# First layer: one latent tile's first products by gathered rows, ahead of the context's; second layer: splits two ahead, gathered sums added at another place

## The chip, the cores and the metric

The kernel runs on one core of one Trainium2 chip. The metric is the device time of one execution in microseconds (us). Engines: TensorE multiplies matrices, VectorE and ScalarE work on tiles, GpSimd does part of the splits and issues the gathers, SyncE issues the other DMAs.

## The reference

Two layers of a diffusion backbone work on 512 latent tokens and 256 context tokens of 1,024 numbers each. Every layer is a norm, a token mixer (attention and recurrences; latents read the context), a residual, a second norm, an expert FFN and a residual. The second layer doesn't need the context's FFN any more, but its mixer needs the context that the first layer's FFN leaves:

```
h = modulate(x, norm_w[layer, 1], sh2, sc2)
s = einsum('nhpd,hpkd->nhpk', (h @ w_q), keys)       # 8 heads, 2 halves, 128 keys each
s_top, i_top = top_k(s, 16)                          # 16 best of each half
best, pos = top_k(s_top[0] + s_top[1], 16)           # 16 of the 256 pairs
idx  = i_top[0] * 128 + i_top[1]  at pos             # one of 16,384 experts
gate = softmax(best)
act  = gelu(einsum('nd,nhkd->nhk', h, u_tab[idx]))
x = x + g2 * einsum('nhk,nhkd->nd', gate * act, v_tab[idx])
```

Each token thus uses 8 x 16 = 128 of 16,384 experts, each with a row of 1,024 in `u_tab` and one in `v_tab`, all in 32-bit floats.

## The kernel before, in words

The FFN is done in two ways beside each other. **Dense**: for a set of latent tokens, all 16,384 experts are computed in 128 steps of 128 experts ("expert j"). A first product (u, lines 1846 to 1856) is 24 matmuls, three for each of eight blocks of 128 numbers, since both operands are split into a high and a low part (`split`: the high part is a rounding copy on ScalarE, L226; the rest is a subtraction on GpSimd or VectorE, L229; lines 246, 247 and 249 are the three matmuls). GELU follows on ScalarE (L1855). Its result is multiplied by the gates that `spread` has placed: one-hot matrices ohA and ohB of the two halves of an expert's number, multiplied on TensorE (L1692) into a staging tile that goes to DRAM (G); ohB is built by VectorE and ScalarE in turn (`OH = "va"`). Most first products are done while the top-k and the spreading run and wait in DRAM (AD): 96 of 128 in the first layer, 80 in the second; the generator `u_step` does one whenever enough "price" has gathered (`UP`). The second products are in `peer_out`: for each expert the activation is weighed by its gates (`weigh`, L1896), split (wh, wl), the row block of values is split (vh, vl), and matmuls add into PSUM (lines 1960 to 1962 in the first layer, whose six accumulators are rolled over every few experts into the latents at L1886; lines 1976 to 1979 in the second). One expert is split ahead of the one that is multiplied.

**By gathers** (`sparse`, lines 1697 to 1739): a tile of 128 tokens has, for each of its 128 chosen experts, one indirect DMA issued by GpSimd that fetches one row for every token (`ga`, 128 x 1024, 0.5 MB), one dot product with the token rows on VectorE (L1727) into a column of `sact`, then GELU, a product with the gate, and again 128 gathers and 128 scaled sums on VectorE (L1737) into `sacc`. `add_tok` transposes sacc on TensorE (L235) and adds it to the stream (L1749); the context's sums pass through DRAM first. The gathers go through a ring of buffers (`NS`: four in the first layer, six in the second, and one more, `NX`, while peer_out runs).

Which tokens go which way: in the first layer (`GT[0] = 0`) all 512 latent tokens are dense and the context's two tiles (256 tokens) are gathered; in the second (`GT[1] = 2`) latents 256 to 511 are gathered and 0 to 255 dense. In the first layer the context's rows are so spread over the latents' dense FFN, and in the second the two gathered tiles over the dense ones.

The order: the program is written as generators. `s.gens` is the list of gathering generators, and `s.pull(n)` takes n steps of the first one in the list; it is called beside the top-k and u_step (`R0`) and after each expert in peer_out (`s.rate`, what is left divided by the experts left). At the end of peer_out `s.pull(1 << 20)` takes all that remains. This program order, with a scheduler that runs the program in a model and arranges each engine's instructions, sets what stands in each engine's queue; an engine takes its queue in order. The gathers carry an anchor (`issue_after`), an instruction behind which they must stand. The stretches of the span are: 950 to 1885 us first products of the first layer, 1885 to 2880 its second products, then the second layer's norm, mixer and retrieval, 3770 to 4330 its first products, 4330 to 5238 its second, and the end.

Names in the rows: `u`, `acc`, `o`, `hs`, `g` are tiles in PSUM (in the rows of L1692 the placed gates); `xl` latents, `xc` context; `htok` token rows; `c_all` constants; `hh`, `hl` the split stream and `whi`, `wlo` the split u-weights; `vraw`, `vh`, `vl` values and their split; `rh`, `rl` the values' last 256 columns, split apart in the first layer.

## Time and profile before

| | |
|---|---|
| median of 3 runs | 5307.02 us (5298.75 to 5309.9) |
| profiled execution | 5302.26 us |
| its span | 5300.4 us |
| mean granted TensorE clock | 0.899 |
| busy: TensorE, VectorE, GpSimd, ScalarE | 4334.2, 4082.6, 2884.6, 1986.3 us |
| first products (lines 246, 247, 249), both layers | 3 x 2048 matmuls, 761.8 + 748.6 + 758.1 us |
| gathers of u-rows, of v-rows | 512, 512 |
| dot products, sums on VectorE | 765.6, 748.6 us |

TensorE has 82% of the span and VectorE 77%, but not in the same places: each stretch has its own bound, so the shares say little, and a table of busy times by stretch says more. The durations of VectorE's and GpSimd's instructions vary with what runs beside them. In rows of groups the second number behind the bar is the mean of one in ns, the idle time is that of the engine just before these instructions, and what ended it stands behind the arrow.

### The profile page before, as it was taken

The numbers are of one execution on the slowest core, as the hardware profiler recorded it, in microseconds if no ns is written. First come the engines' busy times: TensorE is split into PE (matmuls) and PEld (weight loads), VectorE is DVE, ScalarE is ACT, GpSimd is POOL, SyncE is SP. The second block draws the span as 40 slices with busy tenths as digits, with TensorE's granted clock in tenths as the row PEclk, the third lists the DMA queues.
The fourth block names the chain that finished last, engine by engine and source line by source line (L and its number), as shares of the span: only waits on it lengthen the run. The fifth ranks groups of instructions, "written<-read, shape, count | busy, mean of one in ns | idle before, by whom it ended". The sixth has DMA issues, their size and how long they took to land. (4 is left out here: it accounts for less than half of the span.)

```text
span 5300.4 us, 71968 instructions
## 1 busy us (share of the span) xinstructions
PE 4334.2 (82%) x25323; PEld 3508.9 (66%) x25323; DVE 4082.6 (77%) x7744; ACT 1986.3 (37%) x3944; POOL 2884.6 (54%) x1967
## 2 busy tenths in 40 slices
PE   7899988788889978998999998978867765377775
PEld 5777766576668867776777766866756664265563
DVE  4665668899998868777787764644899869977788
ACT  3544442235555632222223463433325542122222
POOL 2232223775567756565654212424566677878775
PEclk8899988899999989999999996989978888688887
DMA  5431124777778888777886110022477789999887
GB/s 201 153 102 62 52 75 154 237 265 248 246 263 306 301 298 292 287 276 274 302 292 230 48 46 9 2 108 97 145 246 248 273 313 358 353 321 331 313 315 277
DMA packets 450409, 1155.52 MB, mean 218 GB/s; under 512 B 42112, under 2 KB 185856, under 8 KB 446464
## 3 DMA queue, kind: packets, MB, share of 16 engines
q1 hardware_dynamic: 302304, 612.94, 33.6%
q0 software_dynamic: 147744, 537.99, 28.2%
q8 instruction: 200, 3.28, 0.2%
q14 instruction: 161, 1.32, 0.1%
HBM read 1052.20 MB, written 98.57 MB: 217 GB/s over the span
## 5 line engine op out<-in xcount | busy, mean ns | idle before, releaser
L229 POOL TENSOR_TENSOR wlo<-wraw,whi 128x1024 fp32r<-128x1024 f32 x405 | 1019.3, 2519 | 1034.6 <-ACT whi L226 999.7
L1715 POOL DMA_INDIRECT ga<-in_pu,idx x512 | 668.6, 1306 | 341.8 <-DVE ga L1727 126.4
L249 PE MATMUL u<-hh,wlo 128*128 128x512 f32 (+1 forms) x2048 | 758.1, 371 | 117.7 <-POOL wlo L229 117.6
L246 PE MATMUL u<-hh,whi 128*128 128x512 f32 (+1 forms) x2048 | 761.8, 372 | 111.6 <-ACT act L1855 74.5
L1737 DVE SCALAR_TENSOR_TENSOR sacc<-ga,sact,sacc 128x1024 f32<-128x1024 f32 x508 | 748.6, 1474 | 107.6 <-DMA ga<-in_pv,idx 99.7
L1727 DVE SCALAR_TENSOR_TENSOR ga<-ga,htok 128x1024 f32<-128x1024 f32 x512 | 765.6, 1511 | 64.2 <-DMA ga<-in_pu,idx 63.9
L1715 POOL DMA_INDIRECT ga<-in_pv,idx x512 | 658.7, 1287 | 264.3 <-DVE sacc L1737 95.0
L226 ACT ACTIVATE whi<-wraw 128x1024 fp32r<-128x1024 f32 x415 | 437.1, 1054 | 859.5 <-PE u L247 469.1
L247 PE MATMUL u<-hl,whi 128*128 128x512 f32 (+1 forms) x2048 | 748.6, 366 | 0.0
L246 PEld LDWEIGHTS u<-hh,whi 128*128 128x128 f32 x2048 | 442.2, 216 | 179.6 <-ACT act L1855 89.5
L249 PEld LDWEIGHTS u<-hh,wlo 128*128 128x128 f32 x2048 | 440.9, 216 | 165.3 <-POOL wlo L229 125.5
L247 PEld LDWEIGHTS u<-hl,whi 128*128 128x128 f32 x2048 | 440.5, 215 | 38.9
L229 DVE TENSOR_TENSOR vl<-vraw,vh 128x768 fp32r<-128x768 f32 (+1 forms) x256 | 349.9, 1369 | 141.3 <-ACT vh L226 141.3
L226 ACT ACTIVATE vh<-vraw 128x768 fp32r<-128x768 f32 (+1 forms) x256 | 239.7, 945 | 287.5 <-PE acc L1961 242.1
L1692 PE MATMUL g<-ohB,ohA 128*128 128x128 f32 x1536 | 253.8, 294 | 111.0 <-DVE ohB L1690 89.5
L1692 PEld LDWEIGHTS g<-ohB,ohA 128*128 128x128 f32 x1536 | 225.2, 201 | 153.4 <-DVE ohB L1690 66.1
L1962 PE MATMUL acc<-wh,vl 128*128 128x512 f32 x768 | 307.7, 401 | 22.6 <-DVE vl L229 22.4
L1960 PE MATMUL acc<-wh,vh 128*128 128x512 f32 x768 | 292.9, 396 | 29.7 <-ACT wh L226 29.7
L1961 PE MATMUL acc<-wl,vh 128*128 128x512 f32 x768 | 305.3, 398 | 8.5 <-POOL wl L229 8.5
L1690 DVE TENSOR_SCALAR ohB<-c_all,pt 128x128 f32<-128x128 f32 x384 | 246.0, 655 | 46.5 <-PE g L1692 46.1
L229 POOL TENSOR_TENSOR wl<-ad,wh 128x512 fp32r<-128x512 f32 (+1 forms) x176 | 214.6, 1219 | 64.4 <-ACT wh L226 30.6
L1855 ACT ACTIVATE act<-u 128x512 f32<-128x512 f32 (+1 forms) x256 | 122.7, 479 | 329.9 <-PE u L249 125.7
(507 smaller groups left out, 9822.6 us busy)
## 6 DMA issues: line engine op xcount, KB each, us to landing
wraw<-in_uT SPq DMA_DIRECT2D x256, 512.0 KB, 4.5
vraw<-in_pv SPq DMA_DIRECT2D x256, 512.0 KB, 6.8
wraw<-in_ada_w SPq DMA_DIRECT2D x96, 512.0 KB, 4.8
G<-stg SPq DMA_DIRECT2D x24, 2048.0 KB, 8.6
wraw<-in_ew SPq DMA_DIRECT2D x64, 512.0 KB, 3.9
G<-G SPq DMA_DIRECT2D x32, 1024.0 KB, 6.7
wraw<-in_pwq SPq DMA_DIRECT2D x48, 512.0 KB, 3.9
AD<-act SPq DMA_DIRECT2D x96, 256.0 KB, 4.6
```

The costliest lines, as they stand in the source:

```text
L226: nc.scalar.activation(hi, x, AF.Copy)
L229: i = (lo_eng or nc.vector).tensor_tensor(lo, x, hi.bitcast(F32), OP.subtract)
L246: nc.tensor.matmul(o, a, hh[:, k], start=(k == 0), stop=False)
L247: nc.tensor.matmul(o, a, hl[:, k], start=False, stop=False)
L249: nc.tensor.matmul(o, b, hh[:, k], start=False, stop=(k == nk - 1))
L1692: nc.tensor.matmul(ps[:, n], A[:, n], B, start=True, stop=True)
L1715: nc.gpsimd.indirect_dma_start(out=ga, out_offset=None, in_=tab, in_offset=bass.IndirectOffsetOnAxis(ap=idx[:, k:k + 1], axis=0))
L1727: nc.vector.scalar_tensor_tensor(ga, ga, 1.0, htok, op0=OP.mult, op1=OP.mult, accum_out=act[:, k:k + 1])
L1737: nc.vector.scalar_tensor_tensor(acc, ga, act[:, k:k + 1], acc, op0=OP.mult, op1=OP.add)
L1960: nc.tensor.matmul(acc[d], a, wh, start=st, stop=False)
L1961: nc.tensor.matmul(acc[d], a, wl, start=False, stop=False)
L1962: nc.tensor.matmul(acc[d], b, wh, start=False, stop=sp)
```

## The change

In the first layer one latent tile, tokens 384 to 511, gets its first products by gathers: 128 gathers of u-rows and 128 dot products (a `sparse` with `half=True`, which ends after GELU and gate). Its own ring has three buffers (`NH`), and its generator is put at the head of `s.gens`, ahead of the context's. The result, gate times activation, goes to `spread` in place of the gate (`halves`, whose ohB all come from VectorE). The dense first products of this layer then cover 384 tokens (`ND`) instead of 512, the second products still 512 (`NW`); `weigh` multiplies 384 columns and uses the other 128 as they were placed. In both layers two tiles have their top-k beside the queries (`NF`; before: one in the first layer). The rings shrink from four and six buffers to three and five (`NS`), the one-hot tiles from six to four (`NE`), and `UP[0]` and `R0[0]` change. In the second layer's second products two experts are split ahead instead of one (`PD`). The sum of its gathered tile that is ready first is transposed and added after expert 101 (`LT = 100`), the other after the last expert; each has a buffer of its own.

```diff
-UP = (5.5, 4.0)
+UP = (4.0, 4.0)
 GT = (0, 2)
-R0 = (2.0, 2.5)
+HT = (1, 0)
+PD = (1, 2)
+R0 = (1.8, 2.5)
 RG = (2, 1)
...
+LT = 100
 RX = 2.0
-NE = 6
+NE = 4
...
-NS = (4, 6)
+NS = (3, 5)
+NF = (2, 2)
+NH = (3, 0)
+TB = 32
...
-    def spread(s, p, p2, p3, sp, psp, gps, pick, tb0, G):
+    def spread(s, p, p2, p3, sp, psp, gps, pick, tb0, G, oh=OH):
...
-                    if OH[c % len(OH)] == 'a':
+                    if oh[c % len(oh)] == 'a':
...
-    def sparse(s, l, p2, pick, src, done):
+    def sparse(s, l, p2, pick, src, done, half=False, pools=None):
...
-        s.nsp += 1
-        q = s.nsp % 2
+        s.nsp += not pools
+        q = 'h' if pools else s.nsp % 2
...
-            s.turn = (s.turn + 1) % len(s.gpools)
-            ga = s.t(s.gpools[s.turn], [128, D], tag='ga')
+            if pools:
+                ga = s.t(s.next_pool(pools), [128, D], tag='ga')
+            else:
+                s.turn = (s.turn + 1) % len(s.gpools)
+                ga = s.t(s.gpools[s.turn], [128, D], tag='ga')
...
-            while len(ahead) < len(s.gpools) and k + len(ahead) < 128:
+            while len(ahead) < len(pools or s.gpools) and k + len(ahead) < 128:
...
-        acc = s.t(p2, [128, D], tag='sacc')
+        if half:
+            done(act)
+            return
+        acc = s.t(p2, [128, D], tag='sacc' if l == 0 else f'sacc{q}')
...
-        ng = GT[l]
-        ND = T - 128 * ng
+        ng, nh = GT[l], HT[l]
+        NW = T - 128 * ng
+        ND = NW - 128 * nh
...
-        tiles = list(range(0, T, 128)) if ctx else list(range(ND, T, 128)) + list(range(0, ND, 128))
+        tiles = list(range(ND, T, 128)) + list(range(0, ND, 128))
...
+            late = []
...
-                    for i in range(ng):
+                    for i in range(ng + nh):
...
+                eg, gated = [], {}
+                if nh and NH[l]:
+                    hs = ee(tc.tile_pool(name=s.name("hs"), bufs=1))
+                    hr = ee(tc.tile_pool(name=s.name("hr"), bufs=NH[l]))
+                def halves():
+                    for i in range(nh):
+                        while i not in gated:
+                            s.pull(1)
+                        pk3 = s.pick[i][0:2] + (gated[i],)
+                        yield from s.spread(*eg, psm, gps, pk3, tiles[i] // TB, G, 'v')
                 def done():
                 def after(i):
                     t0 = tiles[i]
                     if t0 >= ND:
-                        s.todo += 256
-                        s.gens.append(s.sparse(l, s.sp2, s.pick[i], HT[(t0 - ND) // 128],
-                                               lambda acc: s.add_tok(psu, 'u', acc, s.xl, t0, gl)))
-                        next(s.gens[-1])
+                        half = t0 < NW
+                        def end(x):
+                            if half:
+                                gated[i] = x.rearrange("p (a b) -> p a b", a=8)
+                            else:
+                                late.append((x, t0))
+                        s.todo += 128 if half else 256
+                        own = half and NH[l]
+                        g = s.sparse(l, hs if own else s.sp2, s.pick[i], HTok[(t0 - ND) // 128], end, half,
+                                     [hr] * NH[l] if own else None)
+                        s.gens.insert(0 if own else len(s.gens), g)
+                        next(g)
                         return
                     yield from s.spread(*eg, psm, gps, s.pick[i], t0 // TB, G)
                 price, n = 0.0, 0
-                for p in s.retrieve(l, ep, tp_, pk, (psq, 'q'), (psm, 'hs'), (hh, hl), tiles, 1 if ctx else ng, done, after):
+                for p in s.chain([s.retrieve(l, ep, tp_, pk, (psq, 'q'), (psm, 'hs'), (hh, hl), tiles, NF[l],
+                                             done, after), halves()]):
                     price += p
                     if p == 0 and s.gens:
-            s.peer_out(l, ND, old, ap, psu, hd, G, AD, gl)
+            s.peer_out(l, ND, NW, old, ap, psu, hd, G, AD, gl, late)
...
         groups = [list(range(j, j + JG)) for j in range(0, 128, JG)]
...
+        with tc.tile_pool(name=s.name("po"), bufs=2) as p2, tc.tile_pool(name=s.name("pv"), bufs=1 + PD[l]) as pvp, \
+                tc.tile_pool(name=s.name("pw"), bufs=RG[l] + PW + PD[l] - 1) as pw, tc.tile_pool(name=s.name("sp3"), bufs=NX) as sp3, \
...
-                nc.vector.tensor_tensor(a3, a3, G_[:, :, j - g[0], :], OP.mult)
-                return a
+                gj = G_[:, :, j - g[0], :]
+                if ND == NW:
+                    nc.vector.tensor_tensor(a3, a3, gj, OP.mult)
+                    return a3
+                nc.vector.tensor_tensor(gj[:, 0:ND // TB], a3, gj[:, 0:ND // TB], OP.mult)
+                return gj
             def prep(j, a):
-                wh = s.t(pw, [128, ND], F32R, tag='wh')
-                wl = s.t(pw, [128, ND], F32R, tag='wl')
-                s.split(a, wh, wl, lo_eng=nc.gpsimd)
+                wh = s.t(pw, [128, NW], F32R, tag='wh')
+                wl = s.t(pw, [128, NW], F32R, tag='wl')
+                s.split(a, *[x.rearrange("p (b n) -> p b n", n=TB) for x in (wh, wl)], lo_eng=nc.gpsimd)
...
-            a0, a1 = ready(0), ready(1)
-            nxt = prep(todo[0][1], a0)
+            gated = [ready(n) for n in range(PD[l] + 1)]
+            split = [prep(todo[n][1], gated.pop(0)) for n in range(PD[l])]
             pend, cur = [], []
             for n in range(128):
-                (vh, vl), w = nxt
+                (vh, vl), w = split.pop(0)
                 load(n + LA)
                 vload(n + NV)
-                a2 = ready(n + 2)
-                if n + 1 < 128:
-                    nxt = prep(todo[n + 1][1], a1)
-                a1 = a2
+                gated.append(ready(n + PD[l] + 1))
+                if n + PD[l] < 128:
+                    split.append(prep(todo[n + PD[l]][1], gated.pop(0)))
...
-                            nc.tensor.matmul(acc[2 * t + e], b, vh[:, e * 512:e * 512 + 512], start=False, stop=sp)
+                            i = nc.tensor.matmul(acc[2 * t + e], b, vh[:, e * 512:e * 512 + 512], start=False, stop=sp)
+                    if n == LT and late:
+                        a, t0 = late.pop(0)
+                        with tc.issue_after(i.ins):
+                            s.add_tok(psu, 'u', a, s.xl, t0, gl)
                 s.pull(s.rate)
             s.pull(1 << 20)
+            for a, t0 in late:
+                s.add_tok(psu, 'u', a, s.xl, t0, gl)
```

The order of VectorE's instructions at the end of the first layer, before: the last splits of values (L229) and sums of the context (L1737), the last additions to the latents, and the additions of the two context tiles' sums to xc.

```order
L229 TENSOR_TENSOR rl_24331<-vraw_24239,rh_24330 128x256
L1737 SCALAR_TENSOR_TENSOR sacc_20943<-ga_24234,sact_1736_8267,sacc_20943 128x1024
L229 TENSOR_TENSOR vl_24327<-vraw_24239,vh_24326 128x768
...
L1886 SCALAR_TENSOR_TENSOR xl_8281<-u_24380,g_1859_8933,xl_8281 128x512
L1886 SCALAR_TENSOR_TENSOR xl_8281<-u_24388,g_1859_8933,xl_8281 128x512
L1749 SCALAR_TENSOR_TENSOR xc_24419<-o_24432,g_5380_24421,xc_24419 128x128 x4
L1749 SCALAR_TENSOR_TENSOR xc_24419<-o_24441,g_5380_24421,xc_24419 128x128 x4
L1749 SCALAR_TENSOR_TENSOR xc_24419<-o_24452,g_5380_24421,xc_24419 128x128 x4
L1749 SCALAR_TENSOR_TENSOR xc_24419<-o_24461,g_5380_24421,xc_24419 128x128 x4
```

And after: the latents' last additions are at L1923, the context's sums at L1751, the additions to xc at L1763; the second "..." leaves out 89 more sums.

```order
L1923 SCALAR_TENSOR_TENSOR xl_8281<-u_24755,g_1874_8971,xl_8281 128x512
L1751 SCALAR_TENSOR_TENSOR sacc_22181<-ga_22778,sact_1736_8267,sacc_22181 128x1024
L1923 SCALAR_TENSOR_TENSOR xl_8281<-u_24763,g_1874_8971,xl_8281 128x512
L1751 SCALAR_TENSOR_TENSOR sacc_22181<-ga_22814,sact_1736_8267,sacc_22181 128x1024
...
L1751 SCALAR_TENSOR_TENSOR sacc_22181<-ga_22817,sact_1736_8267,sacc_22181 128x1024
L1763 SCALAR_TENSOR_TENSOR xc_24794<-o_24816,g_5529_24796,xc_24794 128x128 x2
L1751 SCALAR_TENSOR_TENSOR sacc_22181<-ga_22859,sact_1736_8267,sacc_22181 128x1024
L1751 SCALAR_TENSOR_TENSOR sacc_22181<-ga_22862,sact_1736_8267,sacc_22181 128x1024
L1751 SCALAR_TENSOR_TENSOR sacc_22181<-ga_22908,sact_1736_8267,sacc_22181 128x1024
...
L1751 SCALAR_TENSOR_TENSOR sacc_22181<-ga_24692,sact_1736_8267,sacc_22181 128x1024
L1763 SCALAR_TENSOR_TENSOR xc_24794<-o_24827,g_5529_24796,xc_24794 128x128 x4
L1763 SCALAR_TENSOR_TENSOR xc_24794<-o_24836,g_5529_24796,xc_24794 128x128 x4
```

Before, the last sums stood among the splits of the last experts and only a few additions followed; after the change 92 sums of one context tile stand in a row behind the last latent addition, and the second context tile's additions (o_24827, o_24836) stand behind them.

TensorE's queue at the same place, before: the last matmul of the last expert (L1884), four times four transposes (L235) of the context's two sums, loaded again as a_5381 and a_5384, and the first matmul of the second layer's norm (L289).

```order
L1884 MATMUL u_24388<-wh_24322,rl_24331 128x512
L235 MATMUL o_24432<-c_all_63,a_5381_24430 128x128 x4
L235 MATMUL o_24441<-c_all_63,a_5381_24430 128x128 x4
L235 MATMUL o_24452<-c_all_63,a_5384_24450 128x128 x4
L235 MATMUL o_24461<-c_all_63,a_5384_24450 128x128 x4
L289 MATMUL hs_24529<-sq_24530,c_all_63 128x256
```

After (L1921, L241 and L295 are these lines' new numbers):

```order
L1921 MATMUL u_24763<-wh_24696,rl_24705 128x512
L241 MATMUL o_24807<-c_all_63,a_5530_24805 128x128 x4
L241 MATMUL o_24816<-c_all_63,a_5530_24805 128x128 x4
L241 MATMUL o_24827<-c_all_63,a_5533_24825 128x128 x4
L241 MATMUL o_24836<-c_all_63,a_5533_24825 128x128 x4
L295 MATMUL hs_24904<-sq_24905,c_all_63 128x256
```

TensorE's order is the same at this place; the transposes still stand ahead of the norm, and the last eight read what the last of the context's sums on VectorE leave.

TensorE's queue in the second layer's second products, where the first gathered tile's sum (`sacc`) is transposed, before: behind the matmuls of an expert (L1979), and ahead of the first product of a later one (L246, L247).

```order
L1979 MATMUL acc_8026_38107<-vh_39307,wl_39304 128x512
L1979 MATMUL acc_8027_38108<-vh_39307,wl_39304 128x512
L235 MATMUL u_39232<-c_all_63,sacc_36984 128x128 x4
L235 MATMUL u_39241<-c_all_63,sacc_36984 128x128 x4
L246 MATMUL u_39269<-hh_31545,whi_39204 128x256
L247 MATMUL u_39269<-hl_31546,whi_39204 128x256
```

After: the transposes (L241) stand behind the matmuls of expert 101 (L2020), and more second products follow (L2017).

```order
L2020 MATMUL acc_8174_38480<-vh_42988,wl_42985 128x512
L2020 MATMUL acc_8175_38481<-vh_42988,wl_42985 128x512
L241 MATMUL u_43063<-c_all_63,sacc_7966_37359 128x128 x4
L241 MATMUL u_43072<-c_all_63,sacc_7966_37359 128x128 x4
L2017 MATMUL acc_8172_38478<-vh_43016,wh_43012 128x512
L2017 MATMUL acc_8173_38479<-vh_43016,wh_43012 128x512
```

The transposes have moved from about a third of the way to a place where the first sum has been complete for long.

VectorE at the end of the second layer, before: sums (L1737) between the last splits of values, and then the last ones of the second tile ahead of its additions to the latents (L1749).

```order
L1737 SCALAR_TENSOR_TENSOR sacc_41526<-ga_43324,sact_6931_33297,sacc_41526 128x1024
L229 TENSOR_TENSOR vl_43775<-vraw_43686,vh_43774 128x1024
L1737 SCALAR_TENSOR_TENSOR sacc_41526<-ga_43358,sact_6931_33297,sacc_41526 128x1024
L229 TENSOR_TENSOR vl_43796<-vraw_43744,vh_43795 128x1024
...
L1737 SCALAR_TENSOR_TENSOR sacc_41526<-ga_43715,sact_6931_33297,sacc_41526 128x1024
L1749 SCALAR_TENSOR_TENSOR xl_8281<-u_43811,g_6588_31818,xl_8281 128x128 x4
```

After: the last split of values, the last six dot products of the second tile (L1738), the product with the gate (L1741), and the first sum (L1749); its other 127 sums follow.

```order
L235 TENSOR_TENSOR vl_44157<-vraw_44127,vh_44156 128x1024
L1738 SCALAR_TENSOR_TENSOR ga_41730,sact_7079_33670<-ga_41730,htok_7080_33671 128x1024
L1738 SCALAR_TENSOR_TENSOR ga_41733,sact_7079_33670<-ga_41733,htok_7080_33671 128x1024
L1738 SCALAR_TENSOR_TENSOR ga_41771,sact_7079_33670<-ga_41771,htok_7080_33671 128x1024
L1738 SCALAR_TENSOR_TENSOR ga_41774,sact_7079_33670<-ga_41774,htok_7080_33671 128x1024
L1738 SCALAR_TENSOR_TENSOR ga_41798,sact_7079_33670<-ga_41798,htok_7080_33671 128x1024
L1738 SCALAR_TENSOR_TENSOR ga_41801,sact_7079_33670<-ga_41801,htok_7080_33671 128x1024
L1741 TENSOR_TENSOR sact_7079_33670<-sact_7079_33670,gate_7031_33472 128x128
L1749 TENSOR_SCALAR sacc_8965_41919<-ga_41920,sact_7079_33670 128x1024
```

Behind the last split of values stood 20 sums, and now six dot products and 128 sums do.

## Rows read from the trace of the kernel before

**Rows 1.** The table of stretches: us, busy time by engine (instructions), clock, DMA

```profile
core 0: us, PE busy (x) PEld busy (x) DVE busy (x) ACT busy (x) POOL busy (x), PEclk, DMA share, GB/s
950.00:1100.00 150.00, 125.26 (x518) 97.53 (x519) 130.30 (x284) 40.91 (x93) 124.29 (x77) 0.85 0.76 255
1100.00:1600.00 500.00, 425.51 (x2004) 348.91 (x2003) 495.45 (x1236) 243.14 (x491) 311.58 (x182) 0.93 0.75 255
1600.00:1885.00 285.00, 258.68 (x1358) 219.94 (x1356) 222.77 (x255) 169.36 (x375) 195.46 (x108) 0.97 0.83 297
1885.00:2880.00 995.00, 913.41 (x3821) 727.08 (x3822) 798.22 (x914) 266.05 (x444) 590.81 (x426) 0.97 0.80 288
4330.00:4480.00 150.00, 105.96 (x427) 82.07 (x428) 121.50 (x108) 44.23 (x65) 111.61 (x87) 0.87 0.97 347
4480.00:4580.00 100.00, 1.57 (x8) 0.98 (x7) 92.15 (x73) 1.06 (x1) 77.38 (x69) 0.53 0.99 373
4580.00:5238.00 658.00, 489.02 (x2130) 389.40 (x2131) 545.95 (x572) 187.88 (x277) 526.07 (x377) 0.86 0.91 326
```

**Rows 2.** The waits, 1885 to 2880 us: who for whom, us, times, longest

```profile
ACT vh L226 <- PE acc L1961: 242.1, 95, 6.1
```

**Rows 3.** TensorE's timeline near 1701 us: start, duration, instruction

```profile
1701.42 0.40 PE L247 MATMUL u<-hl,whi 128*128 128x512 f32 x1
1701.65 0.40 PE L249 MATMUL u<-hh,wlo 128*128 128x512 f32 x1
```

**Rows 4.** TensorE's timeline near 4100 us

```profile
4099.94 0.28 PE L246 MATMUL u<-hh,whi 128*128 128x256 f32 x1
4100.06 0.28 PE L247 MATMUL u<-hl,whi 128*128 128x256 f32 x1
```

**Rows 5.** Three lines' durations: ns, minimum/median/maximum, first and last start in us

```profile
L1727 DVE SCALAR_TENSOR_TENSOR ga<-ga,htok x512: 1195/1214/8399, 959.3 to 4952.0; 128x1024 f32<-128x1024 f32 x171
L1737 DVE SCALAR_TENSOR_TENSOR sacc<-ga,sact,sacc x508: 1257/1285/4046, 1426.9 to 5263.1; 128x1024 f32<-128x1024 f32 x170
L1690 DVE TENSOR_SCALAR ohB<-c_all,pt x384: 286/336/3207, 1205.1 to 4303.5; 128x128 f32<-128x128 f32 x192
```

**Rows 6.** Groups on VectorE, 1100 to 1885 us: busy, mean ns, idle before

```profile
L1690 DVE TENSOR_SCALAR ohB<-c_all,pt 128x128 f32<-128x128 f32 x256 | 155.2, 621 | 15.1 <-PE g L1692 14.9
```

**Rows 7.** Groups on GpSimd, 960 to 1060 us

```profile
L1715 POOL DMA_INDIRECT ga<-in_pu,idx x38 | 55.7, 1466 | 11.6 <-issue 5.8 <-DVE tv L1552 1.4 <-DVE cd L1582 1.1
L229 POOL TENSOR_TENSOR wlo<-wraw,whi 128x1024 fp32r<-128x1024 f32 x10 | 24.3, 2433 | 0.2
```

**Rows 8.** DMA issues, 960-1060 and 4480-4580 us: count, median us to landing

```profile
ga<-in_pu,idx POOLq DMA_INDIRECT x38, 5.9
...
ga<-in_pv,idx POOLq DMA_INDIRECT x64, 6.2
```

**Rows 9.** Groups on GpSimd, 4480 to 4580 us

```profile
L1715 POOL DMA_INDIRECT ga<-in_pv,idx x64 | 72.7, 1136 | 21.3 <-issue 18.0 <-DVE sacc L1737 3.1 <-DMA ga<-in_pv,idx 0.3
```

**Rows 10.** VectorE's timeline, 5230 to 5275 us

```profile
5236.91 1.21 DVE L229 TENSOR_TENSOR vl<-vraw,vh 128x1024 fp32r<-128x1024 f32 x1
5238.05 26.37 DVE L1737 SCALAR_TENSOR_TENSOR sacc<-ga,sact,sacc 128x1024 f32<-128x1024 f32 x20
```

**Rows 11.** TensorE's timeline at two transposes, with the idle time before

```profile
4579.89 1.33 PE L235 MATMUL u<-c_all,sacc 128*128 128x128 f32 x5 [98.43 <-DVE sacc L1737]
...
5264.47 1.97 PE L235 MATMUL u<-c_all,sacc 128*128 128x128 f32 x8 [22.22 <-DVE sacc L1737]
```

**Rows 12.** The waits, 4330 to 5270 us

```profile
ACT wh L226 <- PE acc L1977: 330.1, 100, 12.1
...
DVE vl L229 <- ACT vh L226: 126.3, 51, 9.1
```

**Rows 13.** Groups on VectorE, 4330 to 5270 us

```profile
L1737 DVE SCALAR_TENSOR_TENSOR sacc<-ga,sact,sacc 128x1024 f32<-128x1024 f32 x249 | 350.7, 1408 | 11.8 <-DMA ga<-in_pv,idx 6.5
```

**Rows 14.** The page's groups over the whole span

```profile
L1690 DVE TENSOR_SCALAR ohB<-c_all,pt 128x128 f32<-128x128 f32 x384 | 246.0, 655 | 46.5 <-PE g L1692 46.1
```

25 lines of the change are left out of this document (11 added, 14 removed).

## The prediction, on record before the changed kernel ran

> **What bounds the kernel now.** I read the table of stretches first, then the waits of the two expert stretches, then single durations, and last the order of the built program. In the table [rows 1] the first layer's first products (950 to 1885 us) belong to VectorE: 495.5 of 500 us busy from 1100 to 1600, 848.6 of 935 us over the whole. Its second products (1885 to 2880 us) belong to TensorE: 913.4 of 995 us busy at a granted clock of 0.97, while VectorE works 798.2 us; ScalarE waits 242.1 us there, in 95 waits, for TensorE to give buffers back [rows 2]. In the second layer's second products (4330 to 5238 us, 908 us) VectorE has 759.6 us, GpSimd 715.1 us and the DMA engines a share of 0.91 to 0.99, while TensorE works less than two thirds. Two things stand out there. TensorE stops for 98.4 us, because the transposes of the first gathered sum stand in its queue ahead of the next experts [rows 11]; VectorE stays busy meanwhile (92.2 of 100 us), so the stop isn't lost for it. And VectorE waits 126.3 us for ScalarE's part of a split, which itself waits 330.1 us for TensorE [rows 12]: the split is only one expert ahead.
>
> **The change, part by part.** The sum is made against the profiled execution's own 5302.3 us (span 5300.4, 1.9 us around it); the median of the runs is 4.8 us above that.
>
> A. First layer, first products. A first-product matmul of 512 columns starts every 0.23 us, one of 256 every 0.12 us [rows 3, 4]; I put 384 columns midway, 0.175 us. The 96 experts of this stretch save 96 x 24 x 0.055 = 127 us of TensorE. But VectorE binds here, and it gets more: counted in the built order, 266 dot products and sums of gathered rows stand ahead of the first weighing, where 245 stood, and 64 one-hots come over from ScalarE. At the undisturbed 1.29 us and 0.34 us [rows 5] that is 27 + 22 us: 898 us. Of its 86 idle us, 37 would be left if the stretch kept its length. I take 0. Ends: -28, if VectorE gets the 99% it has from 1100 to 1600 us (898/0.99 = 907), +45 if the 82 idle us outside that stretch stay. Top-k of a second tile beside the queries moves work inside this sum. The change adds one wait: the gathered tile's placing stands behind its last dot product, a GELU and three transposes; behind it in TensorE's queue are only that tile's 128 placing matmuls, and VectorE has context rows to take meanwhile, so nothing is added for it.
>
> The one-hot shows what the undisturbed price hides: median 0.34 us, mean 0.62 us in this stretch [rows 5, 6], with a longest of 3.2 us. The Trainium skill (SBUF — State Buffer, Who interferes with whom) says that a VectorE instruction with two SBUF inputs, or in a two-port mode, and a GpSimd instruction that reads SBUF exclude each other for the whole instruction, so whoever comes second waits it out. By that rule the added work costs its mean and A would be +18 us dearer for the one-hots (64 x 0.28); I keep the median, since the added one-hots stand behind the last weight split.
>
> B. First layer, second products. The 32 remaining first products save 32 x 24 x 0.055 = 42 us on TensorE, which binds. Gathered rows hardly change (274 in the order for 267), nor does VectorE (798 + 9 - some us for narrower weighing). Value -41. Ends: -123, if TensorE never waits (872 us), and +41, if its 82 idle us double. The spilled activations and the one tile held a step longer touch DMA and buffers that aren't short there (share 0.80).
>
> C. The end of the first layer. This is the largest new cost, and only the order shows it (the first two pairs of order rows in the section on the change). 128 more gathered rows must pass through VectorE, and the scheduler hasn't fitted them in: behind the last expert stand 92 sums of the context in one row, where there was none. The transposes of that sum stand in TensorE's queue ahead of every norm of the second layer, and on VectorE the context's additions and norms stand behind the 92. So nothing of the second layer covers them. Price of one: VectorE's own pace is 26.37/20 = 1.32 us [rows 10], when the rows have been fetched already. Here they go through a ring of four buffers. A ring of four gave 38 gathers in 100 us, 2.63 us each, beside weight splits [rows 7]; a ring of seven, with GpSimd doing nothing else, 69 in 100 us, 1.45 us each [rows 1, 9]. Rows land 5.9 to 6.2 us after the issue in both [rows 8], so fewer buffers mean a slower pace. Midway is 2.04 us: 92 x 2.04 = +188 us. Ends: 92 x 1.32 = +121 and 92 x 2.63 = +242.
>
> The Trainium skill (DMA: Bandwidth & Descriptors, Anatomy of one DMA — SWDGE (gpsimd) path) gives a DMA issued by GpSimd about 2.0 us and its bytes at 436 GB/s; an estimate from that for 512 KB is 3.2 us, and four buffers would then feed VectorE at its own pace. No row here is that short: 5.9 us at the median. That result is the fourth rival.
>
> D. Second layer, first products. Four one-hot buffers for six: VectorE's waits of 46.1 us for the placing matmul [rows 14] may grow. Value +8, ends 0 and +46 (the row doubled). Five gather buffers for six cost nothing in this stretch: rows are used far behind their landing.
>
> E. Second layer, second products. The 98.4 us stop goes, since the transposes now stand behind expert 101 (third pair of order rows); 16 transposes are hidden in TensorE's idle time. Splitting two ahead takes ScalarE's wait for TensorE off VectorE. And the stretch loses work: the order has 238 gathered rows up to the last value split where 356 stood. 118 fewer, at 1.41 us on VectorE [rows 13], 1.14 us on GpSimd [rows 9] and 0.52 MB each, leave 593 us, 581 us and 304 - 62 = 242 MB, which at 373 GB/s, the most in the table [rows 1], take 649 us. That is the floor: -259. The ceiling is the old pace without the stop, 908 - 98 = 810 us, less the 49 rows that go from outside it (356 - 69 - 238, at 1.41 us): 741 us, -167. I take 700: -208.
>
> F. The end of the second layer. What left E stands behind the last value split: 6 dot products and 128 sums, where 20 sums took 26.4 us and TensorE waited 22.2 us for them [rows 10, 11]. Its ring has six buffers, near the seven that gave 1.45 us: 134 x 1.45 - 26 = +168. Ends: at 1.32 us +151, at 2.04 us +247.
>
> Sum: 0 - 41 + 188 + 8 - 208 + 168 = +115, so 5302 + 115 = 5417 us.
>
> **Rivals.** 1, faster: gathered rows arrive as fast as VectorE takes them, and freed of 118 of them the second layer's experts run at the DMA floor: -41 + 121 + 8 - 259 + 151 = -20, 5282 us. For it: in the stop VectorE was 92% busy on gathers alone. Against: a DMA share of 1 was only reached there. It decides once E takes under 669 us (-239).
> 2, slower still: the ring sets both ends (2.63 and 2.04 us) and E keeps its old pace: -41 + 242 + 8 - 167 + 247 = +289, 5591 us. For it: rows 7 and 8. Against: the 24 us of weight splits in rows 7, which the ends don't have.
> 3, the first end is hidden behind the second layer's norms: +115 - 188 = -73, 5229 us. Against it stands TensorE's queue.
> 4, both ends at VectorE's pace, the rest as forecast: -41 + 121 + 8 - 208 + 151 = +31, 5333 us. For it: 1.32 us in rows 10; against: those 20 rows had been fetched ahead by seven buffers.
>
> **How the numbers follow.** Forecast 0.55, with a range of its own of 5320 to 5530 (the ends of A to F, added as squares, and a fifth off). Rival 1 0.12, rival 2 0.17, rival 3 0.05, rival 4 0.11. The range 5270 to 5580 leaves out rival 3, a third of rival 1 and about half of rival 2: 0.17. 0.2% of the time is 11 us, about what a measurement can tell from no change. Faster by more: rival 3 and most of rival 1, 0.15. Within: 0.04, from rivals 1 and 4. Slower: 0.81.
>
> **What would show it.** Right: on VectorE, a row of some 92 sums behind the first layer's last expert with TensorE idle beside it, for about 190 us (2 us a sum), and 128 sums at the end with a wait of TensorE near 190 us; no stop of 98 us, and VectorE's wait for ScalarE's value split far under 126 us; second products near 955 us in the first layer, near 700 us in the second. Wrong: C, if those sums go at 1.3 us or something of the second layer runs beside them; E, if the experts still take 740 us, or under 669; A, if the first products shrink by more than 28 us, for then TensorE's saving counted where I let VectorE bind.

## The result and the profile after

The changed kernel takes 5475.14 us (median of 4 runs, 5468.24 to 5491.29), the kernel before 5302.89 us in runs beside it: a ratio of 1.032, 95% interval 1.0294 to 1.0347. The profiled execution spans 5472.2 us, 171.8 more than before. The forecast was 5417 us.

For the comparison I cut both spans at the same six events, read from the timelines: the first dot product, the first and the last second product (`acc`) of the first layer, the first matmul of the second layer's norm, and in the second layer again the first dot product and the first and last second product. The table of stretches of the kernel before, cut so (us, busy time by engine with instructions, granted clock, DMA share, GB/s; the mixer between the layers is left out):

```profile
core 0: us, PE busy (x) PEld busy (x) DVE busy (x) ACT busy (x) POOL busy (x), PEclk, DMA share, GB/s
959.00:1892.00 933.00, 806.33 (x3871) 664.36 (x3869) 850.87 (x1776) 454.01 (x959) 624.90 (x359) 0.93 0.78 267
1892.00:2875.00 983.00, 909.26 (x3801) 723.89 (x3802) 789.99 (x904) 264.30 (x441) 590.81 (x426) 0.97 0.80 289
2875.00:2884.00 9.00, 6.49 (x34) 4.79 (x34) 7.03 (x20) 0.72 (x2) 0.00 (x0) 1.00 0.42 135
3834.00:4337.00 503.00, 336.32 (x2123) 314.33 (x2123) 459.60 (x911) 218.92 (x463) 345.30 (x208) 0.82 0.78 267
4337.00:5242.00 905.00, 600.48 (x2576) 475.43 (x2576) 757.77 (x748) 233.10 (x343) 712.33 (x529) 0.82 0.93 335
5242.00:5300.00 58.00, 16.18 (x42) 7.84 (x40) 37.27 (x54) 8.68 (x14) 11.95 (x12) 0.63 0.42 156
```

The same of the changed kernel:

```profile
970.00:1969.00 999.00, 749.62 (x3876) 686.41 (x3876) 882.41 (x1992) 415.52 (x839) 630.23 (x382) 0.85 0.75 256
1969.00:2861.00 892.00, 850.13 (x3805) 705.49 (x3806) 828.68 (x912) 258.30 (x440) 613.74 (x440) 0.99 0.92 316
2861.00:3057.00 196.00, 6.10 (x30) 4.68 (x29) 130.03 (x116) 0.69 (x2) 112.12 (x94) 0.52 0.81 267
3988.00:4510.00 522.00, 341.62 (x2123) 318.52 (x2124) 468.40 (x918) 227.72 (x466) 356.43 (x213) 0.78 0.79 267
4510.00:5233.00 723.00, 569.83 (x2576) 456.02 (x2575) 607.49 (x621) 230.60 (x340) 561.36 (x406) 0.89 0.93 326
5233.00:5472.00 239.00, 16.55 (x40) 8.13 (x40) 184.69 (x176) 12.53 (x17) 153.81 (x130) 0.52 0.81 296
```

Row by row, by the events' own times (the rows are cut at whole us), the differences are the terms A to F of the prediction: +66, -91, +188, +19, -182, +181 us. What is left of the 171.8, -9 us, is the start (+10) and the mixer between the layers (-19); over all the kernels below these two vary between 949 and 970 us and between 932 and 962 us.

The end of the first layer is the largest. TensorE's timeline there (the number in brackets is the idle time before; [rows 11] are its like):

```profile
3054.34 1.94 PE L241 MATMUL o<-c_all,a 128*128 128x128 f32 x8 [186.23 <-DMA a<-AC]
3056.78 1.65 PE L295 MATMUL hs<-sq,c_all 128*128 128x256 f32 x3 [0.51 <-ACT sq L294]
```

and what VectorE and GpSimd did in those 196 us (groups, answering to [rows 9, 13]):

```profile
L1751 DVE SCALAR_TENSOR_TENSOR sacc<-ga,sact,sacc 128x1024 f32<-128x1024 f32 x96 | 123.3, 1284 | 57.7 <-DMA ga<-in_pv,idx 56.3 <-DVE sacc L1751 0.3
...
L1726 POOL DMA_INDIRECT ga<-in_pv,idx x93 | 112.1, 1206 | 69.1 <-DVE sacc L1751 53.8 <-issue 10.7 <-DMA ga<-in_pv,idx 4.6
```

96 sums take 123.3 + 57.7 = 181 us, 1.89 us each. VectorE waits for the rows to land, and GpSimd waits for VectorE to give a buffer back: a ring that is too small shows itself by these two waits together. At the second layer's end, TensorE's timeline and the two groups:

```profile
5434.44 1.97 PE L241 MATMUL u<-c_all,sacc 128*128 128x128 f32 x8 [201.49 <-DVE sacc L1751]
```

```profile
L1751 DVE SCALAR_TENSOR_TENSOR sacc<-ga,sact,sacc 128x1024 f32<-128x1024 f32 x127 | 163.2, 1285 | 28.2 <-DMA ga<-in_pv,idx 25.0
...
L1726 POOL DMA_INDIRECT ga<-in_pv,idx x128 | 151.6, 1185 | 40.7 <-issue 37.8 <-DMA ga<-in_pv,idx 1.7 <-DVE sacc L1751 1.2
```

Here a sum takes (163.2 + 28.2)/127 = 1.51 us, and GpSimd waits only 2.9 us for others: 1.19 us of issuing and 0.3 us between two issues make 1.5 us. With six buffers it is GpSimd's pace, with four the ring's. The stop of 98.43 us [rows 11] is gone: the first sum's eight transposes follow the matmuls ahead of them without a wait (timeline, first line), and of the waits of [rows 12] these are left:

```profile
5091.47 1.91 PE L241 MATMUL u<-c_all,sacc 128*128 128x128 f32 x8
...
ACT wh L232 <- PE acc L2018: 269.4, 95, 8.3
DVE vl L235 <- ACT vh L232: 90.7, 47, 6.7
```

### The profile page after: what moved, and what is told of

Same layout as the page of the kernel before. It is cut to its first block, busy times and chain, and to the rows that moved or that the text cites. A ratio compares the mean times of both kernels' runs of the same rounds, so it can differ in the third digit from the quotient of the medians.

```text
span 5472.2 us, 72624 instructions
## 1 busy us (share of the span) xinstructions
PE 4190.1 (77%) x25331; PEld 3495.3 (64%) x25331; DVE 4284.9 (78%) x8066; ACT 1951.8 (36%) x3828; POOL 3024.3 (55%) x2095
## 5 line engine op out<-in xcount | busy, mean ns | idle before, releaser
L235 POOL TENSOR_TENSOR wlo<-wraw,whi 128x1024 fp32r<-128x1024 f32 x405 | 996.9, 2465 | 913.9 <-ACT whi L232 876.5
L1751 DVE SCALAR_TENSOR_TENSOR sacc<-ga,sact,sacc 128x1024 f32<-128x1024 f32 x508 | 711.6, 1401 | 112.1 <-DMA ga<-in_pv,idx 104.0
L255 PE MATMUL u<-hh,wlo 128*128 128x384 f32 (+1 forms) x2048 | 692.6, 339 | 117.1 <-POOL wlo L235 116.9
L1738 DVE SCALAR_TENSOR_TENSOR ga<-ga,htok 128x1024 f32<-128x1024 f32 x512 | 732.0, 1443 | 29.7 <-DMA ga<-in_pu,idx 29.3
L252 PE MATMUL u<-hh,whi 128*128 128x384 f32 (+1 forms) x2048 | 687.8, 336 | 71.1 <-ACT act L1892 61.4
L253 PE MATMUL u<-hl,whi 128*128 128x384 f32 (+1 forms) x2048 | 681.0, 333 | 0.0
L1699 PE MATMUL g<-ohB,ohA 128*128 128x128 f32 x1536 | 303.8, 335 | 177.6 <-DVE ohB L1697 127.4
L235 DVE TENSOR_TENSOR vl<-vraw,vh 128x768 fp32r<-128x768 f32 (+1 forms) x256 | 319.6, 1255 | 118.8 <-ACT vh L232 103.9
L1699 PEld LDWEIGHTS g<-ohB,ohA 128*128 128x128 f32 x1536 | 257.9, 232 | 219.2 <-DVE ohB L1697 111.8
L1726 POOL DMA_INDIRECT ga<-in_pu,idxh x128 | 159.5, 1246 | 151.7 <-DVE ga L1738 29.9
L1892 ACT ACTIVATE act<-u 128x384 f32<-128x384 f32 (+1 forms) x256 | 109.5, 428 | 340.7 <-PE u L255 197.0
```

The costliest lines, as they stand in the source:

```text
L235: i = (lo_eng or nc.vector).tensor_tensor(lo, x, hi.bitcast(F32), OP.subtract)
L252: nc.tensor.matmul(o, a, hh[:, k], start=(k == 0), stop=False)
L253: nc.tensor.matmul(o, a, hl[:, k], start=False, stop=False)
L255: nc.tensor.matmul(o, b, hh[:, k], start=False, stop=(k == nk - 1))
L1699: nc.tensor.matmul(ps[:, n], A[:, n], B, start=True, stop=True)
L1726: nc.gpsimd.indirect_dma_start(out=ga, out_offset=None, in_=tab, in_offset=bass.IndirectOffsetOnAxis(ap=idx[:, k:k + 1], axis=0))
```

## The experiments

Stage lengths in us from each profiled execution, cut as above: A to F are the six rows of the tables of stretches, and E+F is the sum of the last two. The ratio is to the kernel before, run beside it on the same chip (5303 to 5316 us there), with its 95% interval.

| kernel | A | B | C | D | E | F | E+F | median | ratio |
|---|---|---|---|---|---|---|---|---|---|
| before | 933 | 983 | 8 | 503 | 905 | 59 | 963 | 5303 | 1 |
| changed | 999 | 892 | 196 | 521 | 723 | 240 | 963 | 5475 | 1.032 (1.0294 to 1.0347) |
| e1 no half tile | 993 | 965 | 8 | 521 | 741 | 228 | 969 | 5379 | 1.0141 (1.0096 to 1.0186) |
| e2 no late addition | 998 | 893 | 195 | 519 | 837 | 121 | 958 | 5478 | 1.0327 (1.027 to 1.0385) |
| e3 one split ahead | 1002 | 888 | 197 | 521 | 733 | 232 | 965 | 5488 | 1.0325 (1.0274 to 1.0376) |
| e4 price of before | 1048 | 897 | 143 | 508 | 725 | 259 | 984 | 5488 | 1.0329 (1.028 to 1.0378) |
| e5 e1, price of before | 1017 | 961 | 8 | 522 | 726 | 234 | 960 | 5380 | 1.0136 (1.0104 to 1.0168) |
| e6 e1, buffers of before | 921 | 948 | 8 | 479 | 704 | 262 | 966 | 5254 | 0.9901 (0.9879 to 0.9924) |
| e7 ring of ten | 931 | 985 | 8 | 501 | 893 | 96 | 989 | 5333 | 1.0038 (1.0017 to 1.006) |
| e8 ring of nine, not late | 932 | 991 | 8 | 504 | 973 | 31 | 1004 | 5358 | 1.0082 (1.0056 to 1.0108) |
| e9 more buffers at both ends | 996 | 877 | 152 | 525 | 816 | 129 | 945 | 5412 | 1.0191 (1.0163 to 1.0218) |
| e10 values loaded twice | 1007 | 896 | 197 | 524 | 793 | 228 | 1021 | 5547 | 1.0439 (1.0413 to 1.0466) |
| e11 e6, one top-k | 917 | 951 | 8 | 498 | 708 | 266 | 974 | 5262 | 0.9909 (0.9883 to 0.9936) |
| e12 e6, one gathered tile | 919 | 954 | 8 | 625 | 721 | 36 | 757 | 5174 | 0.9743 (0.9717 to 0.977) |

The profiled execution of e6 (5218 us) is the fastest of its five; its stages are some 36 us short of its median.

**The half-gathered tile alone (e1).**

```diff
-HT = (1, 0)
+HT = (0, 0)
```

> The changed kernel with HT = (0, 0): all four latent tiles of the first layer dense again, everything else as changed (rings, one-hot tiles, constants, second layer). Theory: in the changed trace the first layer up to the second's first norm costs 173 us more than before (first products +77 with their start, second products -92, the end +188), and all of it comes from the half-gathered tile; the second layer's FFN costs +18 us. So about 5300 us, 5285 to 5330, a span from the first layer's last second product to the next norm under 15 us instead of 196, and a second layer as in the changed kernel (second products near 723 us, the end near 239 us). Rival: the smaller rings and the second layer's new order are what costs; then 5350 us or more.

5379 us: the rival's number. Without the half tile the end C is 8 us again, as the theory had it, but A is still 60 us longer than before, and D 18 us. So the tile itself costs +6 - 73 + 188 = 121 us over A to C (96 us between the medians), and something else in the change costs the rest.

**Price or buffers (e4, e5, e6).** e4 puts the price back in the changed kernel; e5 and e6 start from e1.

```diff
 # e4
-UP = (4.0, 4.0)
+UP = (5.5, 4.0)
 # e5, on e1
-UP = (4.0, 4.0)
+UP = (5.5, 4.0)
-R0 = (1.8, 2.5)
+R0 = (2.0, 2.5)
 # e6, on e1
-NE = 4
+NE = 6
-NS = (3, 5)
+NS = (4, 5)
```

> The changed kernel with the price of a first product in the first layer put back from 4.0 to 5.5, so that the first products are spread over the whole placing instead of ending some 240 us before the second products. The built order has 295 dot products and sums ahead of the first weighing (changed: 266) and 71 behind the last expert (100). Theory: in the changed kernel TensorE has nothing beside the half tile's last dot products and its placing (a wait of 38.5 us and 87 us of placing), and with first products left beside it that time is covered: the first products' stretch falls from 1025 us to some 960 to 1000 us though it holds 29 rows more, the end from 196 to 196 - 29 x 1.92 = 140 us, and the total to 5370 to 5410 us. Rival: VectorE binds there throughout; the stretch grows by 29 x 1.29 = 37 us and only the end gets shorter: 5455 us.

> The first experiment's kernel (HT = (0, 0)) with the first layer's constants UP and R0 of before as well (5.5 and 2.0), rings and one-hot tiles still as changed. In the first experiment the first layer's first products took 993 us with no gathered tile (before: 933, changed: 999), so something else in the change costs 60 us there. Theory: the lower price ends the first products some 120 us ahead of the placing, which then runs alone; with it undone the stretch falls to 935 to 955 us, and the total from 5379 to some 5335 us. Rival: the smaller rings and the four one-hot tiles slow the placing itself (VectorE waits 60.8 us for the placing matmul there, 14.9 before); then the stretch stays at 980 us or more and the total at 5370 us or more.

> The first experiment's kernel (HT = (0, 0)) with six one-hot tiles again and four gather buffers in the first layer (NE = 6, NS = (4, 5)), price and pull as changed. Rival of the run beside it: the rings and one-hot tiles cost the 60 us; then the first products' stretch of the first layer falls to 935 to 955 us, that of the second from 521 to 505 us, and the total to some 5320 us. Theory of the price: the first layer's stretch stays at 980 us or more, and only the second layer's falls by 15 us: 5360 us.

In all three the price as a cause falls. e4 does what its rival said, in kind: 295 rows ahead in place of 266 make A 49 us longer (37 expected) and C 53 us shorter (71 sums left: 143 us, 140 expected), and nothing is won: 5488 us. First products left over didn't cover the tile's placing either; TensorE waits longer for the gathered activation than in the changed kernel (timelines of the changed kernel and of e4):

```profile
1861.22 0.47 PE L241 MATMUL hs<-c_all,sacth 128*128 128x128 f32 x1 [38.49 <-DVE sacth L1741]
...
1899.20 0.47 PE L241 MATMUL hs<-c_all,sacth 128*128 128x128 f32 x1 [81.17 <-DVE sacth L1741]
```

In e5 A grows, to 1017 us. In e6 it falls to 921 us, below before and below the 935 to 955 expected. The two waits that shrink stand on VectorE. Groups of e1, 964 to 1956 us:

```profile
L1697 DVE TENSOR_SCALAR ohB<-c_all,pt 128x128 f32<-128x128 f32 x256 | 163.9, 646 | 61.4 <-PE g L1699 60.8
L1751 DVE SCALAR_TENSOR_TENSOR sacc<-ga,sact,sacc 128x1024 f32<-128x1024 f32 x100 | 159.5, 1595 | 65.2 <-DMA ga<-in_pv,idx 64.0
```

and of e6, 959 to 1880 us:

```profile
L1751 DVE SCALAR_TENSOR_TENSOR sacc<-ga,sact,sacc 128x1024 f32<-128x1024 f32 x101 | 160.3, 1587 | 33.7 <-DMA ga<-in_pv,idx 32.7
L1697 DVE TENSOR_SCALAR ohB<-c_all,pt 128x128 f32<-128x128 f32 x256 | 148.9, 599 | 21.7 <-PE g L1699 21.4
```

39 us less waiting for the placing matmul to free a one-hot tile, and 31 us less for rows to land: 71 of the 72 us by which A differs. It isn't the fast execution of e6 that does it: e11 and e12, with the same sizes, have an A of 917 and 919 us. The two sizes weren't tried apart, nor were they put back beside the half tile.

**The second layer (e2, e3, e7, e8).**

```diff
 # e2 (and e8)
-                                late.append((x, t0))
+                                s.add_tok(psu, 'u', x, s.xl, t0, gl)
 # e3
-PD = (1, 2)
+PD = (1, 1)
 # e7 and e8: HT = (0, 0), UP = (5.5, 4.0), R0 = (2.0, 2.5), NE = 6, NF = (1, 2), and
-NX = 1
+NX = (1, 5)        # e8: (1, 4)
-NS = (3, 5)
+NS = (4, 5)
```

> The changed kernel with the first gathered sum of the second layer transposed and added as soon as it is summed (as before), so behind about the 29th expert in TensorE's queue instead of the 101st; splits stay two ahead. Its built order has 311 gathered rows up to the last value split (changed: 238) and 61 behind it (134). Theory: the stop was never lost for VectorE, the late addition only moves the rows from the stop to the end; so TensorE's stop of some 100 us is back, second products take 723 + 73 x 1.4 = 825 us, the end 239 - 73 x 1.47 = 132 us, and the total is that of the changed kernel, 5475 us, within 15. Rival: the rows fit in beside the experts without lengthening them; then the second products stay near 730 us and the total falls by about 100, to 5375 us.

> The changed kernel with PD = (1, 1): the second layer's splits one expert ahead as before, the late addition kept. Theory: the experts gain their speed from having fewer gathered rows beside them, and the second split ahead took only 36 us off VectorE's wait for ScalarE's value split (126.3 to 90.7 us); so second products of 735 to 760 us instead of 723 and 5485 to 5510 us. Rival 1: gathers and DMA set the pace whatever the split does: 5475 us, within 8. Rival 2: the split ahead is the main gain: second products over 790 us, 5545 us or more.

> First layer as before the change in all its constants; second layer as changed (splits two ahead, first sum added after expert 101) with a ring of ten gather buffers in the second products instead of six, which the scheduler uses to place 340 gathered rows up to the last value split (changed: 238) and 48 behind it (134). The end of the second layer: 239.6 - 86 x 1.47 = 113 us in every theory. Theory: in the experts' stretch VectorE is free for 116 of 723 us, and the DMA engines, at 326 GB/s there, have shown 373; 102 rows more are 53 MB, 289 MB in all: 775 to 833 us, and the total is 5303 - 963 + 888 to 946 = 5228 to 5286 us, faster than before. Rival: the DMA engines give no more than 326 GB/s beside the experts: 887 us, and 5340 us in all. Second rival: VectorE pays 1.41 us for each row: 867 us, 5320 us.

> As the run of ten buffers, but with nine and with the first sum added as soon as it is ready, so that TensorE's stop is back; the built order then has all 388 rows ahead of the last value split and none behind it. The experts' stretch moves 314 MB: 843 us at 373 GB/s, 938 us at the 335 GB/s of before; the end is some 40 us. Theory: a larger ring lets the rows catch up in the stop and the end falls away: between 5223 and 5318 us, and nearer to the run of ten buffers the less the stop costs. Rival: the stop itself is a loss of about 100 us; then it is at least 50 us slower than the run of ten buffers.

e2 is as the theory had it: the stop is back (a wait of TensorE, in e2),

```profile
PE u L241 <- DVE sacc L1751: 104.1, 1, 104.1
```

E is 837 us (825 expected), F 121 (132), and the total that of the changed kernel. In e3 E is 733 us, 10 more than in the changed kernel and just under the theory's 735 to 760, and the total of 5488 us is at the theory's lower end; by its ratio it can't be told from the changed kernel, and E+F is 965 us against 963, so that the first rival isn't excluded. e7 and e8 place 102 and 150 more rows beside the experts and lose what the end gives back. e8, at 5358 us, is above its theory's 5318 and 25 us behind e7, where its rival wanted 50: neither came out. The stretches of e7:

```profile
4345.00:5239.00 894.00, 638.91 (x2576) 491.78 (x2576) 715.80 (x737) 231.94 (x343) 700.71 (x510) 0.81 0.91 326
5239.00:5335.00 96.00, 16.06 (x42) 7.65 (x40) 73.90 (x83) 8.55 (x13) 37.72 (x38) 0.57 0.61 235
```

326 GB/s, as the first rival said, and E+F of 989 us instead of 963. Between e2, e3, e7, e8, before and changed, E+F stays within 958 to 1004 us, wherever 134 rows or none stand behind the last expert. e9 below, with a ring of eight, has 945 us; whether the larger ring gains these 18 us can't be told from one execution of each.

**What sets that sum (e10).** Of a second load of every value block nobody reads anything:

```diff
                     getattr(nc, VQ).dma_start(out=R[j], in_=pv[j])
+                    if l == 1:
+                        x = s.t(rvx, [128, D], tag='vraw2')
+                        getattr(nc, VQ).dma_start(out=x, in_=pv[j])
```

> The changed kernel with every value block of the second layer's second products loaded a second time into a tile that nobody reads (128 x 0.52 MB = 67 MB more, nothing more on the engines). Theory: second products and end together (962 us) are set by the DMA engines, whose busy time there is 866 us in the changed kernel and 866 us in the one before (share times length); 67 MB more at the 322 GB/s of both are 208 us more, so 140 to 210 us and 5615 to 5685 us in all. Rival: VectorE or the ring's round trip sets it; the DMA engines have 96 us free, and the total rises by less than 50 us.

Between the two: E+F rises by 59 us, the median by 72. The experts' stretch of e10:

```profile
4524.00:5317.00 793.00, 598.28 (x2575) 478.12 (x2575) 596.07 (x629) 233.32 (x339) 566.58 (x410) 0.84 1.01 382
```

With the extra bytes the DMA engines do bind (share 1.01, 382 GB/s), but of the 208 us that the bytes would cost at the old rate some 70% found room. So in the changed kernel they are near the limit and not at it. VectorE (792 of 963 us busy over E and F) and GpSimd (715 busy, and 71 us more between its own issues) are near it too. No one of them was shown to set the sum alone; that stays open, and e12, which takes load off all three, doesn't tell them apart.

**The ring at the first layer's end (e9).**

```diff
-NX = 1
+NX = 3
```

> The changed kernel with three more gather buffers instead of one in both layers' second products (NX = 3: six in the first layer, eight in the second). Its built order keeps 95 sums behind the first layer's last expert (changed: 100) and moves 62 rows of the second layer from the end (72 left) to the experts. Theory of the ring: the sums at the first layer's end go at 1.47 us, the pace that six buffers had at the second layer's end, instead of 1.92: 95 x 1.47 + 12 = 152 us instead of 196. Rival: the pace of 1.92 us is the DMA's or GpSimd's own there; the end stays at 185 us or more. Second layer, by the runs so far (second products and end together 958 to 1003 us wherever the rows stood): no gain, 950 to 1000 us. Total by the theory 5420 to 5450 us, by the rival 5475 us.

C is 152 us, as worked out; E+F (945 us) and the total (5412 us) lie 5 and 8 us below what was expected. The groups of e9 from 2826 to 2978 us:

```profile
L1751 DVE SCALAR_TENSOR_TENSOR sacc<-ga,sact,sacc 128x1024 f32<-128x1024 f32 x92 | 118.2, 1285 | 14.7 <-DMA ga<-in_pv,idx 12.6
...
L1726 POOL DMA_INDIRECT ga<-in_pv,idx x88 | 100.9, 1147 | 33.3 <-issue 25.6 <-DVE sacc L1751 7.7
```

(118.2 + 14.7)/92 = 1.44 us a sum, and GpSimd's wait for a buffer is 7.7 us instead of 53.8. With two buffers more the ring no longer limits.

**One top-k beside the queries (e11).**

```diff
 # on e6
-NF = (2, 2)
+NF = (1, 2)
```

> The sixth experiment's kernel (HT = (0, 0), six one-hot tiles, four gather buffers in the first layer; 0.990 of before) with NF = (1, 2): one tile's top-k beside the queries in the first layer, as before, instead of two. Theory, left over by elimination: the second products of the first layer took 948 to 965 us in the three kernels with NF[0] = 2 and all four tiles dense, and 983 to 991 us in the three with 1; so that stretch goes back to some 980 us and the total from 5254 to 5280 us or more. Rival: it is another constant (price, pull or the splits' pools); the stretch stays under 960 us, and the total within 10 of 5254 us.

My elimination was wrong: B stays at 951 us and the total at 5262. The row that goes with B is VectorE's wait for the spilled activations, in e7 (B 985 us) and in e11 (951 us):

```profile
DVE ad L1935 <- DMA ad<-AD: 64.4, 26, 8.3
```

```profile
DVE ad L1935 <- DMA ad<-AD: 29.9, 14, 8.7
```

In the first layer these two differ in price and pull alone. How these make the loads late is open, since e5, with price and pull of before but small rings and two top-k, has a B of 961 us.

So price and pull, though not what costs the 60 us of A, count: A and B together take 1917 us in e7 and 1869 in e11, while before, with the price and pull of e7, took 1916. The 1% by which e6 and e11 are shorter than before comes from the lower price and pull in the first layer; their buffers there are those of before.

**A version faster than both (e12).** If rows in the second layer are dear wherever they stand, the thing to try is fewer of them.

```diff
 # on e6
-GT = (0, 2)
+GT = (0, 1)
-NF = (2, 2)
+NF = (2, 1)
```

> The sixth experiment's kernel with one gathered tile instead of two in the second layer (GT = (0, 1), NF = (2, 1)), so 384 tokens dense there. If the gathered rows' DMA sets the second layer's second products, taking 256 rows (134 MB) away pays more than TensorE's longer matmuls cost: first products of the second layer 600 us instead of 480 to 500 (a third tile to place, 64 us of VectorE, and 39 rows more ahead), second products 730 us at TensorE's pace (128 x 18 matmuls of 0.215 us and 48 x 24 of 0.175 us, at 95%), end 60 us: 1390 us instead of some 1460, and 5185 us in all, 5130 to 5230. Rival: TensorE and VectorE together don't keep that pace, and the gain is lost: 5254 us or more.

5174 us, 0.9743 of before (0.9717 to 0.977). The second layer's first and second products in e12:

```profile
3783.00:4409.00 626.00, 447.73 (x2480) 423.91 (x2481) 586.63 (x1232) 303.30 (x637) 383.58 (x240) 0.88 0.79 268
4409.00:5130.00 721.00, 709.61 (x3334) 612.97 (x3335) 443.80 (x344) 246.47 (x342) 372.70 (x256) 1.00 0.70 238
```

As expected (5185 us). D costs 146 and 122 us more than in e6 and before, but E+F falls from 966 to 757, with TensorE now the bound: 709.6 of 721 us busy, at the full granted clock.

## Why the prediction was right, and where a step failed

The direction and the largest terms were right, and 5475 us lies in the range of the likeliest case (5320 to 5530); the sum was 57 us short. A alone was 66 us off, and B 50 us the other way; that these two nearly cancel is luck. E and F together are 39 us of the 57, D 11.

**C, right.** 188 us were forecast and 188 measured, by the mechanism named: a row of the context's sums behind the last expert, TensorE idle 186.23 us, and a ring of four at 1.89 us a sum. e9 is the proof for the ring. That the two numbers are equal is luck: 2.04 us was a midpoint, and the 181 us measured are 96 sums, not 92, with the transposes and additions around them. Four buffers at 1.89 us are a round trip of 7.6 us, of which the sum itself is 1.3 us and issue and landing 6.3 us. The rule by which four buffers would feed VectorE at its own pace isn't borne out: my estimate of 3.2 us from the Trainium skill (DMA: Bandwidth & Descriptors, Anatomy of one DMA — SWDGE (gpsimd) path) is half of that. Rival 4 falls with it, rival 3 with the 186 us, rival 1 with an E of 723 us (it needed 669), and rival 2 with 1.89 and 1.51 us a sum (2.63 and 2.04).

**F, right; E, right in kind.** F came to +181 (168 forecast), E to -182 (-208). But I summed them to -40, and they are -1: e2 shows the late addition moving some 115 us from one place to the other and no more. The second split ahead, which I listed as part of E's gain, can't be told from no gain (e3), and VectorE's wait for ScalarE's value split fell to 90.7 us only, not "far under 126 us".

**B, within its ends.** -91 us for -41: TensorE's busy time fell by 59 us, not 42, and its idle time from 74 to 42 us. The tile's share of the 91 us is 73 (e1); where the other 18 come from is open. TensorE still binds: ScalarE's wait for it has grown from [rows 2] to this:

```profile
ACT vh L232 <- PE acc L2002: 381.5, 111, 8.2
```

**A, wrong.** Forecast 0, with +45 as the upper end; measured +66. VectorE's busy time rose by 31.5 us to 882 us (898 forecast). The forecast let that work go into the time for which VectorE had been idle, so that 37 us of it would remain, or 82 at the upper end; but the idle time grew from 82 to 117 us. The groups of the changed kernel from 970 to 1969 us:

```profile
L1738 DVE SCALAR_TENSOR_TENSOR ga<-ga,htok 128x1024 f32<-128x1024 f32 x128 | 192.3, 1510 | 16.7 <-DMA ga<-in_pu,idx 16.3
L1738 DVE SCALAR_TENSOR_TENSOR ga<-ga,htokh 128x1024 f32<-128x1024 f32 x128 | 177.2, 1386 | 11.8 <-DMA ga<-in_pu,idxh 10.7 <-issue 0.8
L1697 DVE TENSOR_SCALAR ohB<-c_all,pt 128x128 f32<-128x128 f32 x320 | 169.0, 558 | 61.4 <-PE g L1699 60.2
```

and VectorE's waits for rows in the kernel before, 960 to 1892 us:

```profile
DVE sacc L1737 <- DMA ga<-in_pv,idx: 24.2, 15, 3.9
DVE ga L1727 <- DMA ga<-in_pu,idx: 14.3, 10, 3.4
```

The wait for rows has shrunk, from 38.5 to 27 us; the wait for the placing matmul to free a one-hot tile has grown by 45 us, from 14.9 [rows 6] to 60.2. In A it is 55 to 82 us in all eight kernels with four one-hot tiles and 15 to 21 us in all six with six. The step that failed is thus the one on the buffers, which I put into D alone: "Four one-hot buffers for six: VectorE's waits of 46.1 us for the placing matmul [rows 14] may grow. Value +8." That row is of the whole span, and the first layer places four tiles where the second places two. For the gather ring of three buffers in place of four I charged nothing in A either; in e1 it costs 31 of the 72 us that e6 gives back, but in the changed kernel VectorE doesn't wait longer for rows.

D itself came to +19, and not by its reason: VectorE waits 31.8 us for the placing there, where it waited 31.1; what grew is its busy time, by 9 us, and its wait for rows, from 4 to 17 us. Still, D is 479 to 504 us in the five kernels with six one-hot tiles and two gathered tiles, and 508 to 525 us in the eight with four.

The sentence "nothing is added for it", on the wait for the gathered tile's placing, also failed in what it said: TensorE sat 38.5 us for it in the changed kernel, with no first product left. The 66 us are made up of VectorE's work and waits without it; whether it is one reason why TensorE's saved work bought nothing there isn't shown. The gathered tile's one-hots on VectorE cost what their undisturbed price said, 344 ns in the mean, with 15 gathers and no split on GpSimd beside them (1861 to 1950 us):

```profile
L1697 DVE TENSOR_SCALAR ohB<-c_all,pt 128x128 f32<-128x128 f32 x128 | 37.3, 344 | 11.9 <-PE g L1699 11.4
```

So the higher price from the port rule (the Trainium skill, SBUF — State Buffer, Who interferes with whom) wasn't due here.

## What to carry to other kernels

Where a change needs buffers, charge the ones that it takes from others, in every stretch that uses them: here two one-hot tiles and one gather buffer cost 72 us in one stretch (e1 against e6). A stop of one engine is worth removing only if the engine that works through it has something else to do; when the same rows must pass in any case, they turn up at the end. A ring that feeds an engine wants as many buffers as the round trip holds uses (here 7.6 us at 1.5 us a use, five; four were too few and six enough); its lack shows as two waits at once, the user for the landing and the issuer for a buffer.

## What the runs showed of the hardware

GpSimd's gathers of 0.5 MB came every 1.44 to 1.5 us on average at the two ends with six buffers (1.15 to 1.19 us busy and 0.3 us between). Single ones were faster: in the stop of the kernel before, with seven buffers, they came every 1.32 us for some time (GpSimd's timeline):

```profile
4526.58 1.02 POOL L1715 DMA_INDIRECT ga<-in_pv,idx  x1 [0.30 <-issue]
4527.90 1.02 POOL L1715 DMA_INDIRECT ga<-in_pv,idx  x1 [0.30 <-issue]
```

The DMA engines, which I had put at 373 GB/s at most, gave 382 GB/s at a share of 1.01 in e10. And the mixer between the layers, the same instructions in all kernels, took 932 to 962 us, and was the longer the lower the granted clock of TensorE was in it (0.93 to 0.89). These are its stretches in e5 and in e6:

```profile
2939.00:3899.00 960.00, 842.57 (x7365) 683.28 (x7365) 576.60 (x1668) 401.78 (x861) 317.98 (x269) 0.89 0.20 65
```

```profile
2836.00:3771.00 935.00, 812.68 (x7365) 661.90 (x7365) 577.90 (x1668) 401.85 (x861) 318.01 (x269) 0.93 0.21 67
```

A difference of 20 us between two single executions is therefore no verdict on a change; the ratios above are.
